# Set places for the side steps' matmuls, a rate of 2.9 for the second half's recurrence, one-pass spreads

## The chip, the cores and the metric

The kernel runs on one core of one Trainium2 chip. The metric is the device time of one launch in microseconds, here the median of three runs. The engines are named as in the profile: PE is the matrix engine, PEld its weight loads, DVE the vector engine, ACT the scalar engine, POOL GpSimd, SP the engine that issues many of the DMAs.

## The reference, cut to what matters

One inference step of two layers runs for a prompt of 1024 tokens and for eight sample streams of eight tokens. All weights are shared, all arithmetic is in float32.

```
layer 0:  h = rmsnorm(x);  z = h @ w_in0
          ya = short_conv(z[:, :1536])              # B * conv3(C * h)
          yb = rwkv7(z[:, 1536:])                   # token shift, decay, delta-rule state
          x += concat(ya, yb) @ w_out0
          x += (silu(n @ w_gate) * (n @ w_up)) @ w_down,  n = rmsnorm(x)
layer 1:  the same frame around forgetting attention (prompt, and eight decode streams
          over 2048 cached tokens in pages) and a Mamba-2 scan
y = rmsnorm(x)

rwkv7, per head and token:
          S = S * w_t - (S kk_t) (kk_t a_t)^T + v_t k_t^T ;   o_t = S r_t
          w_t from tanh(wd) @ w2,   a_t from ad @ a2          # two "lora" products, depth 64
```

## The kernel before, in words

The 1088 tokens are split into two halves: `H0` holds the 64 sample tokens and 512 prompt tokens, `H1` the other 512 prompt tokens. Activations lie with features on the partitions.

**Dense work.** A dense product is `gemm_tile` (8 blocks of the inner dimension), and for each block `mm3` (lines 202 to 206), which writes a nearly exact float32 product as three matmuls on rounded operands: high weights by high activations (L204), high by low (L205), low by high (L206). All three use the whole 128x128 array, with 320, 256 or 512 columns. `load_w` brings a weight tile by DMA, ACT rounds it (L196), and POOL or DVE forms the low part (L198).

**Side work.** The recurrence of layer 0 is cut into units of 256 tokens by 2 heads (class `Unit`: `prepare`, `core`, `finish`). Each is a long chain of small matmuls that go back and forth with DVE and ACT. In `core` a triangular matrix is inverted in blocks: `each` (L639) issues 16 matmuls of 32x32 on 16 places of the array, and DVE reads the result. In `prepare`, `small` (L539, L540) makes the lora products: L539 on the whole array and the correction L540 on 64 of its rows. In layer 1 the side work is attention (L1165, L1184, L1192), the paged decode (`decode`: scores L1254 with 128x32 weights, products with the values L1311) and the scan (`ssd`).

**How they are put together.** Both kinds are Python generators. `weave` (lines 485 to 495) takes one step of the dense generator, then as many steps of the side generator as the rate says; what is traced later has a later priority. A scheduler then goes through all instructions: among those that are ready by its own model of the engines it takes the one with the earliest priority, and so fixes the order on every engine. On the chip each engine runs its instructions in that order, and PE has one order for dense and side matmuls.

The weaves, in order: the first half's projection with a norm; `first` (short convolution of `H0`, projection of `H1`) with `recurrence(H0)` at rate 5.5; `second` (output projection and feed-forward of `H0` in layer 0) with `recurrence(H1)` at rate 6; then, in layer 1, `third` and an output feed-forward with attention, scan and decode at rate 1.8; and the last feed-forward with the norms at rate 1.

**Spreads.** A per-token factor that lies on partitions is broadcast and transposed to columns by a float32 matmul against the identity: L255 in `rms`, L838 in `Unit.finish`, L1221 in `decode`. A float32 matmul shows as two records in the trace, one for each of its passes; a matmul on rounded operands, or a transpose (L671), shows as one.

Of the kernel before, what the change touches and what calls it, by code (L numbers as in the profile page):

```python
# [34 lines left out]
CDEC = math.exp(-0.5)  # L35
NEG = -1e30

RATE = (5.5, 6, 1.8, 1.8, 1)

QY = 2  # L40
VY = 3
# [159 lines left out]

def mm3(k, acc, wh, wl, xh, xl, first, last):
    mm = k.nc.tensor.matmul
    mm(acc, wh, xh, start=first, stop=False)  # L204
    mm(acc, wh, xl, start=False, stop=False)  # L205
    mm(acc, wl, xh, start=False, stop=last)  # L206

# [19 lines left out]
def rms(k, H, xs, width, groups=None, ft=None, tag="acc"):  # L227

    nc = k.nc
    ft = ft or (lambda: k.ft(H))  # L230
    groups = groups or H.groups
    lo, hi = groups[0][0], groups[-1][1]
    blocks = [b for b in H.blocks if lo <= b[1] < hi]
    ss = ft()[:, lo:hi]
    for i, x in enumerate(xs):
        sq = ft()[:, lo:hi] if i else ss
        nc.scalar.activation(sq, x[:, lo:hi], AF.Square)  # L237
        if i:
            nc.vector.tensor_add(ss, ss, sq)  # L239
        if i % 2:  # L240
            yield
    pt = k.bank(tag)
    nb = len(blocks)
    for j, (l, _, _) in enumerate(blocks):
        nc.tensor.matmul(pt[:, j:j + 1], ss[:, l - lo:l - lo + P], k.con("ones"), start=True, stop=True)  # L245
    r = k.bp.tile([P, 16], F32, name="rs", tag="rs", bufs=2)
    nc.vector.tensor_scalar(r[:, 8:8 + nb], pt[:, :nb], 1.0 / width, EPS, op0=ALU.mult, op1=ALU.add)
    rsqrt(k, r[:, 0:nb], r[:, 8:8 + nb])
    yield
    out = []  # L250
    for a, b in groups:
        pb = k.bank(tag)
        for j, (_, c, w) in enumerate(blocks):
            if a <= c < b:
                nc.tensor.matmul(pb[:, c - a:c - a + w], r[:, j:j + 1].to_broadcast([P, P]), k.con("ident")[:, :w], start=True, stop=True)  # L255
        out.append((a, b, pb[:, :b - a]))
    yield
    return out
# [22 lines left out]
class Even:  # L281
    def __init__(self, k, pool):
        nc, A = k.nc, k.A
        self.k, self.mp = k, pool
        self.st_sc = pool.tile([P, 4, 16], F32, name="st_sc")
        nc.sync.dma_start(self.st_sc, A["st_sc"])
        self.st_shift = pool.tile([P, 14, 8], F32, name="st_shift")
        nc.sync.dma_start(self.st_shift, A["st_shift"])
        self.o_sc = pool.tile([P, 4, 18], F32, name="o_sc")
        nc.gpsimd.memset(self.o_sc, 0.0)  # L290
        self.o_shift = pool.tile([P, 14, 9], F32, name="o_shift")
        nc.gpsimd.memset(self.o_shift, 0.0)
        k.load_con(pool, 1)

        self.lora = [pool.tile([P, 512], F32R, name="lora%d" % i) for i in range(3)]
        raw = self.tile([P, 512], "up")
        for i, t in enumerate(self.lora):
            for c in range(2):
                nc.sync.dma_start(raw[64 * c:64 * c + 64], A["lora"][64 * (i if i < 2 else c):64 * (i if i < 2 else c) + 64])
            nc.scalar.copy(t, raw)  # L300
            if i == 2:
                nc.vector.tensor_sub(t, raw, t)
        self.g2 = pool.tile([P, 512], F32, name="g2")
        nc.sync.dma_start(self.g2, A["rw_g2"])
        self.reset = pool.tile([P, 512], F32, name="reset")
        nc.sync.dma_start(self.reset, A["resets"][0:1, 0:512].to_broadcast([P, 512]))
        self.dv = pool.tile([P, 30], F32, name="dv")
        dv = self.dv
        nc.vector.tensor_scalar(dv[:, 0:14], k.pp[:, PP["mu"]:PP["mu"] + 14], -1.0, 1.0, op0=ALU.mult, op1=ALU.add)
        for o, n, f in ((14, "w0", 0.5), (18, "a0", 0.5), (22, "ka", 0.5), (26, "kk", -0.5)):  # L310
            nc.vector.tensor_scalar(dv[:, o:o + 4], k.pp[:, PP[n]:PP[n] + 4], f, None, op0=ALU.mult)
        self.krz = [pool.tile([P, 4, 128], F32, name="krz%d" % h) for h in range(2)]
        for h in range(2):
            nc.gpsimd.memset(self.krz[h][64 * (1 - h):64 * (2 - h)], 0.0)
        self.state = []
        for p in range(4):
            s = pool.tile([P, 64], F32, name="S", tag="S%d" % p, bufs=2)
            nc.gpsimd.memset(s, 0.0)
            self.state.append(s)
# [162 lines left out]
        yield  # L482


def weave(dense, side, rate, rest=True):

    due = 0.0
    for _ in dense:
        due += rate
        while due >= 1:  # L490
            due -= 1
            if next(side, True) and not rest:
                return
    if rest:
        drain(side)
# [6 lines left out]
class Unit:  # L502
# [18 lines left out]
    def prepare(self):  # L521
# [8 lines left out]
        def small(c):  # L530

            z = la if c == 0 else self.et("la")
            nc.sync.dma_start(z[:, :n], k.zl[self.H.i][c][:, self.ts])
            z = z[:, :n].bitcast(F32R)
            o = k.bank()
            hs = slice(64 * c, 64 * c + 64)
            for sl, i in cols:
                f = slice(128 * i, 128 * i + 128)
                mm(o[:, sl], m.lora[c][:, f], z, start=True, stop=False)  # L539
                mm(o[:, sl], m.lora[2][hs, f], z[hs], start=False, stop=True)  # L540
            return o

        for j, x in ((1, xk), (0, xr), (2, xv)):
# [266 lines left out]
    def finish(self):  # L810
# [24 lines left out]
        yield  # L835
        pr = k.bank()
        for j in range(2):
            mm(pr[:, 128 * j:128 * j + 128], s2[:, 128 * j:128 * j + 128], k.con("ident"), start=True, stop=True)  # L838
        for sl, i in cols:
            V.scalar_tensor_tensor(oo[:, sl], oo[:, sl], k.col("lnw", i), pr[:, sl], op0=ALU.mult, op1=ALU.mult)  # L840
        yield
# [82 lines left out]
class Odd:  # L924
# [271 lines left out]
    def decode(self):  # L1196
# [6 lines left out]
        with k.tc.tile_pool(name="fd", bufs=1) as dp:  # L1203
# [7 lines left out]
            for p in range(4):  # L1211
                d = slice(32 * p, 32 * p + 32)
                sm = [tl([P, NS], "sm", 3) for _ in range(3)]
                for t, src in zip(sm, (k.qd, k.kd, k.vd[0])):
                    nc.sync.dma_start(t, src[p][:, 0:NS])
                for r in range(4):
                    e = slice(32 * r, 32 * r + 32)
                    V.tensor_copy(ksp[d, r], sm[1][e])
                    V.tensor_copy(qsp[d, r, :, p], by8(sm[0][e]))
                pt = k.bank()  # L1220
                mm(pt[0:64, 0:128], sm[2], k.con("ident"), start=True, stop=True)  # L1221
                S.copy(vs[:, 128 * p:128 * p + 128], pt[0:64, 0:128])
            cq = tl([P, 4], "cq")
            ncn = tl([P, NS], "ncnr")
# [292 lines left out]
def hybrid_step(tc, A, O):  # L1517
    nc = tc.nc
    k = K()
    k.nc, k.tc, k.A, k.O, k.cc = nc, tc, A, O, {}  # L1520
    k.low = nc.gpsimd
    with ExitStack() as es:
        cp = es.enter_context(tc.tile_pool(name="cp", bufs=1))
        dp = es.enter_context(tc.tile_pool(name="dp", bufs=1, space=DRAM))
# [33 lines left out]
        with tc.tile_pool(name="m0", bufs=1) as mp, tc.tile_pool(name="mps", bufs=1, space=PSUM) as k.mps:  # L1558
            norm = rms_split(k, H0, x0, "nm0")
            next(norm)  # L1560
            m = Even(k, mp)
            h0 = drain(norm)
            h1 = []

            def first():
                yield from m.short_conv(H0, h0)
                yield from m.project(H1, h1)
                yield from islice(conv1, CF[0])

            def norm1():  # L1570
                h1.extend((yield from rms_split(k, H1, x_in(H1), "nm0")))

            weave(m.project(H0, h0), norm1(), 1)
            x0 = []
            conv1 = m.short_conv(H1, h1)

            def second():
                x0.extend((yield from ffn0(H0, islice(conv1, CF[1]))))

            weave(first(), m.recurrence(H0), RATE[0])  # L1580
            weave(second(), m.recurrence(H1), RATE[1])
            h0 = drain(beside(rms_split(k, H0, x0, "nm1"), conv1))
            drain(conv1)
            m.finish()
        with tc.tile_pool(name="m1", bufs=1) as mp, tc.tile_pool(name="mps1", bufs=1, space=PSUM) as k.mps:
            m = Odd(k, mp)
            drain(m.dense(H0, h0))

            x2 = []

            def third():
                x1 = yield from ffn0(H1)
                h = yield from rms_split(k, H1, x1, "nm1")
                yield from m.dense(H1, h)

            ffn = keep(out_ffn(k, F0, 1), x2)
            k.low = nc.vector
            side = chain(m.latency(H0), m.latency(H1))
            weave(third(), side, RATE[2], False)
            weave(ffn, side, RATE[3], False)  # L1600
            k.low = nc.gpsimd
            drain(side)
            m.finish()
        with tc.tile_pool(name="x1", bufs=1) as k.xp:
            ffn1 = out_ffn(k, F1, 1, last=lambda xs, a, b: final(F1, xs, [(a, b)]))
            weave(ffn, islice(ffn1, 20), RATE[4])
            weave(ffn1, final(F0, x2), 1)


def scratch(k, dp):  # L1610
# [122 lines left out]
```

## Time and profile before

| | |
|---|---|
| median of three runs | 3324.24 us (3321.57 to 3326.07) |
| the profiled execution's own time | 3320.28 us |
| its span | 3318.5 us |
| PE busy | 3133.4 us, 94% of the span, 25213 records |
| PE weight loads | 2652.5 us, 80% |
| DVE busy | 1901.8 us, 57% |
| ACT busy | 1056.3 us, 32% |
| POOL busy | 839.8 us, 25% |
| mean granted clock of PE | 0.972 |

PE is the busiest engine by far, and the other engines serve it. Busy time says little of how well PE is used: matmuls are pipelined, so the records of neighbours overlap, and what a matmul costs is read from its start to the start of the next one.

### The profile page before, as it was taken

What the parts mean: (1) busy time and instruction counts of PE and PEld (TensorE: products, weight loads), DVE (VectorE), ACT (ScalarE), POOL (GpSimd) and SP (SyncE); (2) the same over time, 40 slices, a digit from 0 to 9 for tenths busy, and PEclk for the clock granted to TensorE, in tenths of its full rate; (3) what the DMA queues carried; (4) which work ended last, traced back from release to release, by engine and by line L of the source; (5) the groups of instructions that cost most, each with busy time, mean ns of one, the idle gap of its engine ahead of it and who ended that gap; (6) DMA issues with size and microseconds to landing.
All of it is one profiled execution on the core that took longest, in us unless ns stands there. A gap on an engine that the chain in (4) does not pass through costs nothing. (4 is left out here: it accounts for less than half of the span.)

```text
span 3318.5 us, 63244 instructions
## 1 busy us (share of the span) xinstructions
PE 3133.4 (94%) x25213; PEld 2652.5 (80%) x25213; DVE 1901.8 (57%) x3603; ACT 1056.3 (32%) x2083; POOL 839.8 (25%) x561
## 2 busy tenths in 40 slices
PE   7999999999999998999999998989999998999998
PEld 6877657777889997987677775766777776899998
DVE  6766646565544447566666466565545666544445
ACT  4333323332222223345322223332224553322222
POOL 3423333332323333310400103002010002433332
PEclk9999999999999998999999998999999998999999
DMA  5312233211112234643445656875544334232222
GB/s 179 117 59 80 88 92 122 68 60 56 57 61 83 83 104 128 212 153 102 144 143 167 203 155 209 252 225 176 171 166 148 111 106 152 70 109 83 82 80 78
DMA packets 238471, 409.20 MB, mean 123 GB/s; under 512 B 37632, under 2 KB 129664, under 8 KB 238176
## 3 DMA queue, kind: packets, MB, share of 16 engines
q10 hardware_dynamic: 63232, 218.80, 20.3%
q1 hardware_dynamic: 165584, 152.27, 15.4%
q0 software_dynamic: 9360, 34.08, 3.0%
q8 instruction: 199, 3.26, 0.4%
q14 instruction: 96, 0.79, 0.1%
HBM read 352.23 MB, written 52.81 MB: 122 GB/s over the span
## 5 line engine op out<-in xcount | busy, mean ns | idle before, releaser
L204 PE MATMUL acc<-hh,wh 128*128 128x320 f32 (+2 forms) x3720 | 1264.1, 341 | 19.0 <-ACT hh L218 15.3
L206 PE MATMUL acc<-hh,wl 128*128 128x320 f32 (+2 forms) x3720 | 1255.4, 338 | 6.3 <-POOL wl L198 6.2
L205 PE MATMUL acc<-hl,wh 128*128 128x320 f32 (+2 forms) x3720 | 1256.5, 338 | 4.6 <-DVE hl L219 3.6
L198 POOL TENSOR_TENSOR wl<-wraw,wh 128x1024 fp32r<-128x1024 f32 x225 | 540.1, 2401 | 1011.2 <-ACT wh L196 957.8
L204 PEld LDWEIGHTS acc<-hh,wh 128*128 128x128 f32 x3720 | 713.4, 192 | 98.9 <-ACT hh L218 20.5
L196 ACT CAST wh<-wraw 128x1024 fp32r<-128x1024 f32 (+1 forms) x398 | 416.0, 1045 | 1142.0 <-PE acc L205 1036.0
L205 PEld LDWEIGHTS acc<-hl,wh 128*128 128x128 f32 x3720 | 715.2, 192 | 70.4 <-DVE hl L219 6.9
L206 PEld LDWEIGHTS acc<-hh,wl 128*128 128x128 f32 x3720 | 714.6, 192 | 69.8 <-POOL wl L198 8.3
L903 DVE TENSOR_TENSOR x<-x,acc 128x320 f32<-128x320 f32 (+2 forms) x528 | 270.5, 528 | 142.5 <-PE acc L206 141.2
L205 PE MATMUL acc<-hidl,wh 128*128 128x320 f32 (+2 forms) x1056 | 352.0, 334 | 0.2 <-DVE hidl L219 0.2
L204 PE MATMUL acc<-hidh,wh 128*128 128x320 f32 (+2 forms) x1056 | 347.8, 336 | 3.8 <-ACT hidh L218 1.9
L206 PE MATMUL acc<-hidh,wl 128*128 128x320 f32 (+2 forms) x1056 | 348.6, 332 | 0.0
L198 DVE TENSOR_TENSOR wl<-wraw,wh 128x1024 fp32r<-128x1024 f32 x173 | 211.0, 1220 | 135.6 <-ACT wh L196 127.1
L1318 POOL DMA_INDIRECT kv<-in_cv,vidx x64 | 74.0, 1156 | 619.8 <-DMA kv<-in_ck 487.8
L204 PEld LDWEIGHTS acc<-hidh,wh 128*128 128x128 f32 x1056 | 198.7, 189 | 26.6 <-ACT hidh L218 4.5
L205 PEld LDWEIGHTS acc<-hidl,wh 128*128 128x128 f32 x1056 | 199.6, 189 | 18.0 <-issue 1.4
L206 PEld LDWEIGHTS acc<-hidh,wl 128*128 128x128 f32 x1056 | 199.8, 189 | 15.5 <-issue 1.0
L219 DVE TENSOR_TENSOR hidl<-ft,hidh 128x512 fp32r<-128x512 f32 (+2 forms) x148 | 177.1, 1196 | 57.0 <-ACT hidh L218 52.7
L891 DVE SCALAR_TENSOR_TENSOR ft<-ft,acc 128x320 f32<-128x320 f32 (+2 forms) x132 | 70.1, 531 | 205.9 <-PE acc L206 205.7
L885 DVE SCALAR_TENSOR_TENSOR ft<-ft,acc 128x320 f32<-128x320 f32 (+2 forms) x132 | 69.7, 528 | 177.7 <-ACT ft L884 177.6
L218 ACT CAST hidh<-ft 128x512 fp32r<-128x512 f32 (+2 forms) x148 | 75.2, 508 | 117.8 <-DVE ft L891 114.7
L1430 POOL TENSOR_TENSOR ac<-ac,bc 128x576 f32<-128x576 f32 (+1 forms) x16 | 27.2, 1710 | 292.2 <-DMA wraw<-in_wg 256.3
(344 smaller groups left out, 3314.1 us busy)
## 6 DMA issues: line engine op xcount, KB each, us to landing
wraw<-in_wi ACTq DMA_DIRECT2D x100, 512.0 KB
wraw<-in_wg ACTq DMA_DIRECT2D x88, 512.0 KB
wraw<-in_wu ACTq DMA_DIRECT2D x88, 512.0 KB
wraw<-in_wd ACTq DMA_DIRECT2D x88, 512.0 KB
kv<-in_ck SPq DMA_DIRECT2D x512, 64.0 KB
wraw<-in_wo ACTq DMA_DIRECT2D x32, 512.0 KB
ka<-kp SPq DMA_DIRECT2D x48, 128.0 KB
x<-in_xT SPq DMA_DIRECT2D x16, 288.0 KB
```

Source lines behind the costliest of these rows:

```text
L196: nc.scalar.copy(wh, raw)
L198: k.low.tensor_sub(wl, raw, wh)
L204: mm(acc, wh, xh, start=first, stop=False)
L205: mm(acc, wh, xl, start=False, stop=False)
L206: mm(acc, wl, xh, start=False, stop=last)
L218: k.nc.scalar.copy(hh, v)
L219: (eng or k.nc.vector).tensor_sub(hl, v, hh)
L885: nc.vector.scalar_tensor_tensor(s[:, a:b], s[:, a:b], 1.0, pc, op0=ALU.add, op1=ALU.mult)
L891: nc.vector.scalar_tensor_tensor(s[:, a:b], s[:, a:b], 0.5, pu, op0=ALU.mult, op1=ALU.mult)
L903: nc.vector.tensor_add(xs[n][:, a:b], xs[n][:, a:b], acc[:, :b - a])
L1318: nc.gpsimd.indirect_dma_start(out=v, out_offset=None, in_=A["cv"].rearrange("o (s r) c -> (o s) (r c)", r=2), in_offset=bass.IndirectOffs ...
L1430: G.tensor_mul(t, t, bc[2 + g])
```

## The change

`mm3` now notes each first matmul in `k.log`. `weave` asks, after each dense step, how many priorities it took (`back`) and which first matmuls it logged (`new`). If n side steps are due, the j-th is traced with its priorities moved back to the start of that dense step, and its PE instructions are put in the order behind the logged matmul number len(new)*j/n. That is an order on PE's queue alone, with no semaphore. The rate of the second half's recurrence goes from 6 to 2.9.

The correction of the lora products gets a fourth tile: tiles 2 and 3 hold the low part in their own 64 rows and zeros in the other 64, so that L540 uses all 128 rows. The three spreads become transposes.

```
-RATE = (5.5, 6, 1.8, 1.8, 1)
+RATE = (5.5, 2.9, 1.8, 1.8, 1)
...
-    mm(acc, wh, xh, start=first, stop=False)
+    k.log.append(mm(acc, wh, xh, start=first, stop=False))
...
-                nc.tensor.matmul(pb[:, c - a:c - a + w], r[:, j:j + 1].to_broadcast([P, P]), k.con("ident")[:, :w], start=True, stop=True)
+                nc.tensor.transpose(pb[:, c - a:c - a + P], r[:, j:j + 1].to_broadcast([P, P]), k.con("ident"))
...
-def weave(dense, side, rate, rest=True):
+def weave(k, dense, side, rate, rest=True):
...
     due = 0.0
-    for _ in dense:
+    while True:
+        p0, n0 = k.tc.cur_priority, len(k.log)
+        if next(dense, True):
+            break
+        back, new = k.tc.cur_priority - p0, k.log[n0:]
         due += rate
-        while due >= 1:
-            due -= 1
-            if next(side, True) and not rest:
+        n = int(due)
+        due -= n
+        for j in range(n):
+            with k.tc.issue_after(new[len(new) * j // n].ins) if new else nullcontext(), k.tc.high_priority(offset=back):
+                over = next(side, True)
+            if over and not rest:
                 return
...
-                mm(o[:, sl], m.lora[2][hs, f], z[hs], start=False, stop=True)
+                mm(o[:, sl], m.lora[2 + c][:, f], z, start=False, stop=True)
...
-            mm(pr[:, 128 * j:128 * j + 128], s2[:, 128 * j:128 * j + 128], k.con("ident"), start=True, stop=True)
+            nc.tensor.transpose(pr[:, 128 * j:128 * j + 128], s2[:, 128 * j:128 * j + 128], k.con("ident"))
...
-                mm(pt[0:64, 0:128], sm[2], k.con("ident"), start=True, stop=True)
+                nc.tensor.transpose(pt[0:64, 0:128], sm[2], k.con("ident"))
```

In the order of the built programs, PE comes to a matmul on a part of the array (a "small tile") out of other work 553 times before and 1252 times after the change; the number of dense matmuls, 14328, and of side matmuls, 5861, is the same. By line (numbers of the kernel before): L639 from 109 to 562, L1254 from 31 to 152, L1311 from 40 to 97, L540 from 40 to none, and all other lines from 333 to 441. The last matmul of the second half's recurrence stood behind 3198 dense matmuls and now stands behind 5257; `second` ends with the 5352nd.

On PE, in the second half's recurrence, before (L639 is one level of the block inverse, on tile `rk`; the rows with `acc` are the dense product around it):

```order
L204 MATMUL acc_6859<-hh_6485,wh_6827 128x256
L205 MATMUL acc_6859<-hl_6493,wh_6827 128x256
L639 MATMUL rk_6641<-t0_6639,nt_6621 32x32 x16
L206 MATMUL acc_6859<-hh_6485,wl_6829 128x256
L204 MATMUL acc_6993<-hh_6478,wh_6987 128x320
```

The same kind of level on PE in the changed program, later in the feed-forward (L652 is the former L639):

```order
L204 MATMUL acc_11728<-hidh_11310,wh_11724 128x320
L652 MATMUL rk_11794<-t0_11792,nt_11575 32x32 x3
L205 MATMUL acc_11728<-hidl_11311,wh_11724 128x320
L652 MATMUL rk_11794<-t0_11792,nt_11575 32x32
L206 MATMUL acc_11728<-hidh_11310,wl_11726 128x320
L652 MATMUL rk_11794<-t0_11792,nt_11575 32x32
L204 MATMUL acc_11728<-hidh_11482,wh_11724 128x320
L652 MATMUL rk_11794<-t0_11792,nt_11575 32x32
L205 MATMUL acc_11728<-hidl_11483,wh_11724 128x320
```

The 16 matmuls stood together between two dense matmuls; now dense and side matmuls take turns. Other levels still stand together.

On PE, in the paged decode, before (L1254 makes the scores of one page, on tile `fs`):

```order
L206 MATMUL acc_21624<-hh_17606,wl_21622 128x512
L1254 MATMUL fs_21588<-kt_21679,qsp_19152 32x128 x8
L1254 MATMUL fs_21588<-kt_21616,qsp_19152 32x128 x8
L204 MATMUL acc_21705<-hh_17599,wh_21699 128x512
L205 MATMUL acc_21705<-hl_17607,wh_21699 128x512
```

And in the changed program (L1267 is the former L1254):

```order
L204 MATMUL acc_21329<-hh_17609,wh_21325 128x512
L1267 MATMUL fs_21293<-kt_21384,qsp_19157 32x128
L205 MATMUL acc_21329<-hl_17617,wh_21325 128x512
L1267 MATMUL fs_21293<-kt_21384,qsp_19157 32x128
L206 MATMUL acc_21329<-hh_17609,wl_21327 128x512
L1267 MATMUL fs_21293<-kt_21384,qsp_19157 32x128
L204 MATMUL acc_21329<-hh_17610,wh_21325 128x512
```

Here too a page's scores went between two dense matmuls as a whole; now they take turns with them one by one. On the other engines the rows hardly change in number (DVE 3412 to 3431, ACT 2305 to 2307, POOL 551 to 546, SP 1969 to 1972).

## Rows read from the trace of the kernel before

**Rows 1.** The page, part 1: engine, busy us, share of the span, instructions.
```profile
PE 3133.4 (94%) x25213; PEld 2652.5 (80%) x25213; DVE 1901.8 (57%) x3603; ACT 1056.3 (32%) x2083; POOL 839.8 (25%) x561
```

**Rows 2.** Stretches of the three weaves with side work: length, busy, clock.
```profile
core 0: us, PE busy (x) PEld busy (x) DVE busy (x) ACT busy (x) POOL busy (x), PEclk, DMA share, GB/s
127.80:512.60 384.80, 359.12 (x4774) 274.52 (x4773) 238.79 (x622) 121.72 (x325) 125.48 (x110) 0.96 0.29 86
512.60:1242.80 730.20, 696.98 (x7138) 625.07 (x7137) 385.87 (x838) 202.38 (x431) 239.45 (x147) 0.98 0.23 75
...
1411.10:2838.40 1427.30, 1359.24 (x8163) 1047.67 (x8162) 856.77 (x1404) 492.06 (x926) 181.01 (x150) 0.97 0.52 163
```

**Rows 3.** Timeline, second weave, one small matmul between dense ones: start, us, instruction.
```profile
607.26 0.31 PE L205 MATMUL acc<-hl,wh 128*128 128x320 f32 x1
...
607.40 0.31 PE L206 MATMUL acc<-hh,wl 128*128 128x320 f32 x1
607.64 0.24 PE L700 MATMUL rk<-tt,wm 32*32 32x32 f32 x2
...
608.16 0.32 PEld L700 LDWEIGHTS rk<-tt,wm 32*32 32x32 f32 x14 [0.16 <-issue]
608.16 0.43 PE L700 MATMUL rk<-tt,wm 32*32 32x32 f32 x14
```

**Rows 4.** Timeline of PE, second weave: a level of 16 matmuls that stand together.
```profile
595.48 0.45 PE L639 MATMUL rk<-t,nt 32*32 32x32 f32 x32
595.86 0.42 PE L204 MATMUL acc<-hh,wh 128*128 128x320 f32 x1
596.11 0.31 PE L205 MATMUL acc<-hl,wh 128*128 128x320 f32 x1
```

**Rows 5.** Timeline of PE, decode: one 128x64 matmul between dense ones.
```profile
1696.72 0.40 PE L205 MATMUL acc<-hidl,wh 128*128 128x512 f32 x1
1696.96 0.40 PE L206 MATMUL acc<-hidh,wl 128*128 128x512 f32 x1
1697.29 0.43 PE L1221 MATMUL rk<-con,sm 128*64 128x128 f32 x2
1697.65 0.50 PE L204 MATMUL acc<-hidh,wh 128*128 128x512 f32 x1
```

**Rows 6.** Timeline of PE, decode: the 16 score matmuls of a page, together.
```profile
1748.19 1.08 PE L1254 MATMUL fs<-kt,qsp 128*32 128x128 f32 x32
1749.21 0.51 PE L204 MATMUL acc<-hh,wh 128*128 128x512 f32 x1
1749.55 0.39 PE L205 MATMUL acc<-hl,wh 128*128 128x512 f32 x1
```

**Rows 7.** Timeline of PE, decode: eight products with the values, together.
```profile
1881.58 1.07 PE L1311 MATMUL rk<-kv,pd 128*32 128x256 f32 x16
1882.58 0.50 PE L204 MATMUL acc<-hh,wh 128*128 128x512 f32 x1
```

**Rows 8.** Timeline of PE, first weave: a lora product and its correction.
```profile
306.64 0.28 PE L539 MATMUL rk<-la,lora 128*128 128x256 f32 x1
306.85 0.38 PE L540 MATMUL rk<-la,lora 64*128 64x256 f32 x1
...
307.50 0.40 PE L204 MATMUL acc<-hh,wh 128*128 128x512 f32 x1
```

**Rows 9.** Timeline of PE, first weave: float32 passes of 128 columns on the whole array.
```profile
303.27 1.16 PE L622 MATMUL rk<-krz,kb 128*128 128x128 f32 x8 [0.45 <-DVE o_shift L398]
304.27 1.06 PE L622 MATMUL rk<-kr,kb 128*128 128x128 f32 x8
```

**Rows 10.** Groups by line, PE, 127.8 to 2838.4 us: records | busy, mean ns | idle before.
```profile
L838 PE MATMUL rk<-con,s 128*128 128x128 f32 x68 | 12.1, 302 | 4.8 <-DVE s L834 3.7 <-ACT vu L682 0.9 <-DVE tt L665 0.3
```

**Rows 11.** Two stretches of 3.4 us in the second weave, columns as in Rows 2.
```profile
706.70:710.10 3.40, 1.96 (x65) 1.26 (x68) 3.40 (x9) 0.59 (x3) 1.03 (x1) 1.00 0.64 171
710.10:713.50 3.40, 3.40 (x69) 2.99 (x59) 1.64 (x8) 0.46 (x1) 0.00 (x0) 0.50 0.27 99
```

More of the change, by code (lines that the diff above doesn't have):

```diff
@@ L293, in __init__ @@
         k.load_con(pool, 1)
-        self.lora = [pool.tile([P, 512], F32R, name="lora%d" % i) for i in range(3)]
+        self.lora = [pool.tile([P, 512], F32R, name="lora%d" % i) for i in range(4)]
         raw = self.tile([P, 512], "up")
-        for i, t in enumerate(self.lora):
+        for i, t in enumerate(self.lora[:3]):
             for c in range(2):
@@ L301, in __init__ @@
             if i == 2:
-                nc.vector.tensor_sub(t, raw, t)
+                for c in range(2):
+                    hs = slice(64 * c, 64 * c + 64)
+                    nc.vector.tensor_sub(self.lora[2 + c][hs], raw[hs], t[hs])
+                nc.vector.memset(raw, 0.0)
+                for c in range(2):
+                    hs = slice(64 * c, 64 * c + 64)
+                    nc.scalar.copy(self.lora[3 - c][hs], raw[hs])
         self.g2 = pool.tile([P, 512], F32, name="g2")
@@ L535, in small @@
             o = k.bank()
-            hs = slice(64 * c, 64 * c + 64)
             for sl, i in cols:
@@ L1521, in hybrid_step @@
     k.low = nc.gpsimd
+    k.log = []
     with ExitStack() as es:
@@ L1571, in norm1 @@
                 h1.extend((yield from rms_split(k, H1, x_in(H1), "nm0")))
-            weave(m.project(H0, h0), norm1(), 1)
+            weave(k, m.project(H0, h0), norm1(), 1)
             x0 = []
@@ L1578, in second @@
                 x0.extend((yield from ffn0(H0, islice(conv1, CF[1]))))
-            weave(first(), m.recurrence(H0), RATE[0])
-            weave(second(), m.recurrence(H1), RATE[1])
+            weave(k, first(), m.recurrence(H0), RATE[0])
+            weave(k, second(), m.recurrence(H1), RATE[1])
             h0 = drain(beside(rms_split(k, H0, x0, "nm1"), conv1))
@@ L1598, in hybrid_step @@
             side = chain(m.latency(H0), m.latency(H1))
-            weave(third(), side, RATE[2], False)
-            weave(ffn, side, RATE[3], False)
+            weave(k, third(), side, RATE[2], False)
+            weave(k, ffn, side, RATE[3], False)
             k.low = nc.gpsimd
@@ L1605, in hybrid_step @@
             ffn1 = out_ffn(k, F1, 1, last=lambda xs, a, b: final(F1, xs, [(a, b)]))
-            weave(ffn, islice(ffn1, 20), RATE[4])
-            weave(ffn1, final(F0, x2), 1)
+            weave(k, ffn, islice(ffn1, 20), RATE[4])
+            weave(k, ffn1, final(F0, x2), 1)
 def scratch(k, dp):
```

## The prediction

> **What bounds the kernel now.** I read the busy table first, then the weaves as stretches, then the timeline of PE around single side matmuls, and last the clock. PE is busy for 94% of the span, the next engine for 80% (PE's own weight loads) and DVE for 57% [rows 1]: whatever lengthens PE's own queue lengthens the run, unless it fills time in which PE waits. How much of that there is, the stretches show [rows 2]: PE is idle for 384.8 - 359.1 = 25.7 us in the first weave with a recurrence, 33.2 in the second and 68.1 in layer 1, together 127 us. The granted clock there is 0.96, 0.98 and 0.97; at half clock half the time is lost, so the shortfalls 0.04 x 384.8, 0.02 x 730.2 and 0.03 x 1427.3 make 15 + 15 + 43 = 73 us. Waiting and slow clock are thus worth 200 us at most in the stretches that the change touches. Some waiting can hide in busy records, since the ends of matmuls are modelled; I keep that for the range.
>
> The decisive rows are those of one small matmul among dense ones. Two dense matmuls of 320 columns start 0.14 to 0.15 us apart (607.26, 607.40). Before a small one the distance is 0.24 (607.40 to 607.64). From there to the next small one, with one dense matmul between, it is 0.52 (607.64 to 608.16) [rows 3]. So one 32x32 matmul that stands alone costs 0.52 - 0.147 = 0.37 us of PE, with nothing waiting in it. Sixteen that stand together cost little more: 0.24 - 0.147 = 0.09 to get in, 0.38 to get back to a dense matmul, and 0.25 - 0.147 = 0.10 more on that one: 0.57 us [rows 3, 4]. PE pays for leaving the dense stream and coming back, not for the small matmuls.
>
> **The change part by part.** PE leaves for a small tile 553 times before and 1252 times after, 699 more, by the built order. For side matmuls on the whole array an extra place costs nothing that I can see, and I price none.
>
> 1. The block inverse (L639): 453 more. Sixteen alone cost 16 x 0.37 = 5.92 us against 0.57 together, 0.357 for each of the 15 that were added: 453 x 0.357 = +162 us. Bounds: the halves of a level, or three together, cost less for each; 0.30 gives 136, 0.37 gives 168.
>
> 2. The scores of the decode (L1254): 121 more. The trace has none alone; the nearest row is a 128x64 matmul of as many columns between dense ones of 512: in at 1696.96 to 1697.29 (0.33 against 0.24 for two dense ones, 0.09), 0.36 until the next dense one [rows 5], and 0.34 - 0.24 = 0.10 more on that [rows 6]: 0.55 us. Sixteen together cost 1.02 + 0.09 + 0.10 = 1.21 [rows 6]. That is (16 x 0.55 - 1.21) / 15 = 0.51 each, 121 x 0.51 = +62 us. If the narrower weights come in as fast as those of the 32x32 matmul, it is 0.37 alone and (5.92 - 1.21) / 15 = 0.31 each, +38.
>
> 3. The products with the values (L1311): 57 more, none alone in the trace. They have twice the columns of the 128x64 row, so at least its 0.55; eight together cost 1.00 + 0.19 [rows 5 to 7]. (8 x 0.55 - 1.19) / 7 = 0.46; I take 0.5, 57 x 0.5 = +28 us, between 0.3 and 0.65 (17 to 37).
>
> 4. The other small-tile lines: 333 entries before, 441 after, 108 more. They are mostly pieces of two to four matmuls, cheaper per piece: I take 0.3, +32 us, between 0 (they fall where PE waited) and 40.
>
> 5. The lora correction on all rows: 40 entries go. A product and its correction take from 306.64 to 307.50, 0.86 us, of which one dense matmul of 512 columns is 0.24 [rows 5, 8]; two of 256 columns on the whole array take at most two of the 320-column distances, 0.29. That is 0.33 saved, about 0.37 at 256 columns: 40 x 0.37 = -15 us; eight of them have only 64 columns, so -10 is the other bound. The zeros are written before the first weave, beside dense work: 0, at worst +2.
>
> 6. One-pass spreads: L838 shows 68 records for its 34 matmuls [rows 10], and the spreads of the norms lose 54 passes too. A pass of 128 columns on the whole array takes 1.00 us / 8 = 0.125 [rows 9]: 88 x 0.125 = -11 us; the four in the decode are within the rounding.
>
> Work added on PE: 162 + 62 + 28 + 32 - 15 - 11 = +258 us.
>
> 7. Waiting. The places are an order on PE's queue and no new wait: behind each side matmul stands a dense one. The chains get longer (a level of the inverse at one matmul per 0.52 us takes 8 us in place of 0.57), so DVE's reading of a level, and what stands behind it there, comes later. At the new pace there is room: the last matmul of that recurrence stands behind dense matmul 5257 of 5352, so nothing is left to drain. Of the idle time I give back three quarters in the second weave, whose pace is halved (-25 us), and a third in the other two, whose rates stay (-31); with some waiting that hides in busy records I take -70. Bounds: 0, and all 127. The clock I leave as it is: 0, between -73 and +60 (third rival).
>
> Sum on the profiled execution's own time: 3320.3 + 258 - 70 = 3508 us, of which the span is all but 2 us. The median of the runs is 4 us above that execution: 3512 us forecast.
>
> **The rivals.** *Faster: coming back costs nothing.* If weights for the next matmul are loaded while the last one streams, small and dense matmuls alternate freely, and only the gains are left: 3324 - 70 - 15 - 11 = 3228, and down to 3180 if more waiting goes. It decides if an alternating pair takes 0.15 + 0.05 us in place of 0.52. Against it: the weight load of L700 starts at 608.16 together with its matmul, 0.52 us behind the last start of that kind, and "issue" says that it waited for nothing that the profile shows; it was not pulled under the dense matmul [rows 3]. [...]
>
> *Even: waiting eats the whole cost.* If nearly all idle time and half of the slow clock go (-165), and the pieces fall at the lower ends (136 + 38 + 17 + 0 - 15 - 11 = 165), the time is 3324; at the middle prices it is 3417. For it: PE waits in just these stretches. Against it: the rates of two of three weaves are the same, and 127 us of idle is half of what is added.
>
> *Slower still: the clock falls in the alternating stretches.* There 453 periods of 0.52 and 178 of about 0.79 us (0.55 + 0.24) make 377 us in which PE streams few columns. The clock fell to half behind a stretch in which PE was at work for 1.96 of 3.40 us on small matmuls [rows 11]. If a third of the 377 us runs at half clock and half of each period scales with it, that is 377 / 3 x 0.5 = +63 us: 3575, and 3620 with no waiting recovered. [...]
>
> *The change does not do what it says:* if PE's order on the chip were another than the built one. Nothing speaks for it; PE runs its queue in order.
>
> **How the numbers follow.** The forecast, with its own bounds (terms 1 to 7 at their ends), 0.70, between 3430 and 3580. The clock falls, 0.14, 3575 to 3640. The even rival 0.11, 3317 to 3430; of this 0.02 lies within 0.2% of 3324 (3317.6 to 3330.9), which is about what a measurement of this kernel can tell from no change, and 0.01 below. The faster rival 0.05. So faster 0.06, same 0.02, slower 0.92. The range for 8 in 10 takes the forecast's bounds, most of the clock's case above and the upper part of the even one below: 3400 to 3615.
>
> **What would show it.** In the profile after: records of L652 of two at a time, alternating with dense rows at about 0.52 us from one to the next; the stretch of the second weave near 730 + 80 us, the first near 385 + 35, layer 1's near 1427 + 75; PE's idle time in them down by half, while PE's busy share rises above 94% though the run is longer. About 90 fewer records on PE. The prediction is wrong if alternating rows stand 0.2 to 0.3 us apart, or if the second weave is no longer than 760 us; its size is wrong if the granted clock leaves 0.95 to 0.99.

## The result, and the profile after

The changed kernel takes 3676.7 us (median of 4 runs, 3665.49 to 3691.95); the kernel before, timed beside it, 3325.15 (4 runs, 3321.57 to 3326.63). The ratio is 1.107 [1.104, 1.110]: 352 us slower, where 188 were forecast (3512), and outside the range given (3400 to 3615). The direction was right, the size was not.

The page of the changed kernel, engines and the row of the granted clock:

```profile
PE 3523.8 (96%) x25121; PEld 2817.5 (77%) x25121; DVE 1899.4 (52%) x3605; ACT 1064.5 (29%) x2085; POOL 835.6 (23%) x561
PEclk9977898988878888999989999899999999999999
```

PE has 92 records fewer than before [rows 1] and is busy 390 us longer; DVE, ACT and POOL do the same work as before. The clock row is the second thing to see: its sevens and most of its eights stand in the first 40% of the span, which is where the two recurrences run.

The stretches of the three weaves in the changed kernel (columns: length, busy time of each engine with its instructions, granted clock, DMA share, GB/s; the last row is layer 1):

```profile
128.30:594.10 465.80, 444.65 (x4777) 318.69 (x4775) 243.66 (x643) 128.44 (x334) 128.62 (x115) 0.87 0.24 74
594.10:1496.20 902.10, 888.37 (x7099) 735.36 (x7100) 377.01 (x830) 204.17 (x432) 240.64 (x146) 0.86 0.19 59
...
1662.40:3195.20 1532.80, 1469.34 (x8070) 1054.05 (x8069) 856.42 (x1400) 491.34 (x924) 170.41 (x149) 0.97 0.49 151
```

Against [rows 2] the first weave is 81 us longer (384.8 to 465.8) and the second 172 (730.2 to 902.1). Layer 1 now ends its stretch at an earlier dense matmul (8070 PE records against 8163); before, the stretch to the same matmul is this one:

```profile
1411.10:2829.20 1418.10, 1350.04 (x8094) 1038.47 (x8093) 850.63 (x1399) 490.43 (x924) 176.65 (x149) 0.97 0.52 163
```

so layer 1 is 115 us longer (1532.8 against 1418.1). PE's idle time in the three went from 25.7, 33.2 and 68.1 us to 21.2, 13.7 and 63.5. The clock went from 0.96 and 0.98 to 0.87 and 0.86 in the two recurrences, and stayed at 0.97 in layer 1.

### The profile page after: what moved, and what is told of

Same layout as the page of the kernel before. It is cut to its first block, busy times and chain, and to the rows that moved or that the text cites. A ratio compares the mean times of both kernels' runs of the same rounds, so it can differ in the third digit from the quotient of the medians.

```text
span 3682.6 us, 62973 instructions
## 1 busy us (share of the span) xinstructions
PE 3523.8 (96%) x25121; PEld 2817.5 (77%) x25121; DVE 1899.4 (52%) x3605; ACT 1064.5 (29%) x2085; POOL 835.6 (23%) x561
## 5 line engine op out<-in xcount | busy, mean ns | idle before, releaser
L205 PE MATMUL acc<-hl,wh 128*128 128x320 f32 (+2 forms) x3720 | 1318.7, 355 | 7.8 <-DVE hl L219 5.9
L204 PE MATMUL acc<-hh,wh 128*128 128x320 f32 (+2 forms) x3720 | 1300.4, 351 | 26.2 <-ACT hh L218 20.5
L206 PE MATMUL acc<-hh,wl 128*128 128x320 f32 (+2 forms) x3720 | 1299.8, 350 | 4.2 <-POOL wl L198 4.0
L204 PEld LDWEIGHTS acc<-hh,wh 128*128 128x128 f32 x3720 | 734.0, 198 | 110.9 <-ACT hh L218 25.1
L205 PEld LDWEIGHTS acc<-hl,wh 128*128 128x128 f32 x3720 | 733.3, 197 | 100.3 <-issue 24.8
L206 PEld LDWEIGHTS acc<-hh,wl 128*128 128x128 f32 x3720 | 734.0, 197 | 82.8 <-issue 19.8
L205 PE MATMUL acc<-hidl,wh 128*128 128x320 f32 (+2 forms) x1056 | 368.2, 349 | 0.5 <-DVE hidl L219 0.5
L206 PE MATMUL acc<-hidh,wl 128*128 128x320 f32 (+2 forms) x1056 | 364.3, 346 | 0.0
L204 PE MATMUL acc<-hidh,wh 128*128 128x320 f32 (+2 forms) x1056 | 359.9, 347 | 1.1 <-DVE x L916 0.5
L652 PEld LDWEIGHTS rk<-t,nt 32*32 32x32 f32 x2112 | 65.7, 112 | 85.2 <-issue 72.0
```

The lines of the kernel that those rows point to most:

```text
L204: k.log.append(mm(acc, wh, xh, start=first, stop=False))
L652: mm(o[q, 32 * c:32 * c + 32], lhs[q, c], rhs[q, c], start=True, stop=True)
```

## The experiments

All of them compute the full result. "Entries" are the times PE comes to a small tile out of other work, counted in the built order; by the count used for these runs the changed kernel has 1242 (1252 ahead of the prediction). A count of PE's records in the traces lies higher for every kernel but keeps the distances within a few: 1335 for the changed kernel, 599 for experiment 1 and 1371 for experiment 2, which are counted as 1242, 509 and 1278 here. In `weave`, a side step is given the scheduling priority that the dense step began with (`offset=back`), and that is undone behind each side step. So the side step whose place is at the first dense matmul has the same priorities as the dense matmuls themselves, one by one, and the scheduler lets them take turns; side steps with later places come out together.

The theory to test: the whole loss comes from taking turns, that is, from the price of an entry and from the clock that falls there. Under the rivals, the set places or the slower pace cost the time, whether or not the matmuls take turns.

**1. The same places and pace, with side matmuls together.**

```diff
-  ... k.tc.high_priority(offset=back):
+  ... k.tc.high_priority(offset=back + 300):
```

> The changed kernel with one number altered: the side steps' priorities go 300 further back than the start of the dense step, so that a side step's matmuls stand before the dense ones as soon as they are ready and behind their set place, and no longer take turns with them. PE comes to a small tile 509 times by the built order (553 before the change, about 1250 with it). Theory A (the cost is the taking of turns: about 0.36 us for each time PE leaves the dense stream, and the clock that falls in the alternating stretches): nothing of the loss is left, the granted clock is 0.96 or more in both recurrences, and the time is 3240 to 3310 us. Rival B (the cost comes from the moved priorities, which let side work on DVE, ACT and POOL pass the dense work's evictions and weight preparation): that is kept here, and the time stays above 3550. Rival C (the pace of 2.9 costs): also kept, above 3450.

Measured: 3296.01 us (3294.61 to 3299.04), ratio to before 0.993 [0.990, 0.995], with 509 entries. Its weaves (same columns):

```profile
129.90:517.50 387.60, 352.21 (x4779) 273.11 (x4777) 244.25 (x650) 127.77 (x339) 131.91 (x118) 0.96 0.29 91
517.50:1206.80 689.30, 673.73 (x7097) 613.01 (x7098) 382.57 (x823) 201.97 (x427) 237.49 (x143) 0.98 0.23 76
1373.20:2807.00 1433.80, 1350.15 (x8069) 1036.19 (x8068) 856.84 (x1400) 491.43 (x924) 167.20 (x149) 0.97 0.51 162
```

And PE's timeline around a level of the block inverse (start, length, instruction):

```profile
702.54 0.45 PE L652 MATMUL rk<-t,nt 32*32 32x32 f32 x32
702.92 0.41 PE L205 MATMUL acc<-hidl,wh 128*128 128x320 f32 x1
```

One number in the priorities takes away all of the loss, 381 us: the sixteen matmuls of a level stand together again, in one row of 32 records (two for each). The clock is back at 0.96 and 0.98, and the second weave is 41 us shorter than before [rows 2]. The rivals fell: neither the places nor the pace cost much. What the turns cost is 902.1 - 689.3 = 213 us in the second weave, 78 in the first and 99 in layer 1.

**2. Turns with three dense matmuls between lone small ones.** The changed kernel, with one line behind each small matmul of the block inverse:

```diff
     mm(o[q, 32 * c:32 * c + 32], lhs[q, c], rhs[q, c], start=True, stop=True)
+    k.tc.cur_priority += 2
```

> The changed kernel, with the priority moved on by two more after each 32x32 matmul of the block inverse: about as many lone small matmuls (1278 entries against about 1250), but most with three dense matmuls between them in place of one. Theory A, which puts 160 us of the loss down to the clock and the rest to leaving the dense stream: the granted clock of the two recurrences goes from 0.87 and 0.86 back to 0.94 or more, with the price of 0.36 us for each lone matmul still paid: 3500 to 3570 us. If the clock were a by-product of waiting and the whole loss were paid for leaving the dense stream (0.5 us and more for each): 3650 to 3700.

Measured: 3593.81 us (3580.43 to 3598.26), ratio 1.083 [1.080, 1.085], with 1278 entries, 36 more than in the changed kernel. Its two recurrences, and its timeline of PE:

```profile
127.50:548.50 421.00, 397.50 (x4758) 287.50 (x4758) 243.98 (x633) 129.23 (x335) 128.21 (x113) 0.98 0.26 80
548.50:1394.30 845.80, 824.89 (x7118) 677.10 (x7117) 384.37 (x840) 203.31 (x431) 239.87 (x147) 0.98 0.20 64
```

```profile
703.43 0.24 PE L652 MATMUL rk<-t,nt 32*32 32x32 f32 x2
703.61 0.50 PE L205 MATMUL acc<-hl,wh 128*128 128x512 f32 x1
703.95 0.39 PE L206 MATMUL acc<-hh,wl 128*128 128x512 f32 x1
704.18 0.39 PE L204 MATMUL acc<-hh,wh 128*128 128x512 f32 x1
704.50 0.24 PE L652 MATMUL rk<-t,nt 32*32 32x32 f32 x2
```

Most of the lone matmuls now have three dense ones between them, as these do. The clock is 0.98 in both, and no entry was saved. That separates the two parts. The price of an entry, from this run and the first: (3593.8 - 3296.0) / (1278 - 509) = 0.387 us, an average over all kinds of entries, net of the waiting that they fill. The clock: the changed kernel is 82.9 us slower than this one with 36 entries fewer, 82.9 + 36 x 0.387 = 97 us. The run is 24 us over the upper end of what was expected.

**3. Turns with two dense matmuls between.** The same line with `+= 1`.

> As the kernel that leaves three dense matmuls between lone 32x32 matmuls, with two (1315 entries to small tiles, 635 in the block inverse). [...] If the clock only follows the number of entries: 0.87 as in the changed kernel, and 3680 to 3720 us.

Measured: 3636.14 us (3632.78 to 3649.9), ratio 1.096 [1.094, 1.099], 1315 entries. Its recurrences:

```profile
127.20:577.90 450.70, 426.80 (x4778) 308.44 (x4776) 245.32 (x645) 128.73 (x335) 131.49 (x115) 0.92 0.25 77
577.90:1445.00 867.10, 855.78 (x7097) 692.48 (x7098) 378.22 (x829) 203.29 (x430) 238.03 (x145) 0.94 0.19 61
```

With one, two and three dense matmuls between, the second weave's clock is 0.86, 0.94 and 0.98. The author's estimate ahead of the run was a clock of 0.95 or more and 3590 to 3625 us if the second dense matmul were enough; the run came out between that and the time by entries alone. At 0.387 an entry it stands 3636.1 - 3593.8 - 37 x 0.387 = 28 us above the run with three: the part of the clock that is still lost.

**4. All side steps take turns.**

```diff
-  ... k.tc.high_priority(offset=back):
+  ... k.tc.high_priority(offset=back - back * j // n):
```

> The changed kernel with every side step's priorities starting at its own set place, so that nearly all of them take turns with the dense matmuls: 1818 entries to small tiles against about 1250, 902 in the block inverse against 562. The suspected cost, raised. Theory A: 340 more lone 32x32 matmuls at 0.385 us and as much again of the clock as the 453 cost (0.26 each), 219 us, and some 230 other entries at 0.3 to 0.5, 70 to 115: 3965 to 4010 us, granted clock of the recurrences at 0.80 or less. If PE hides entries beyond those that wait: below 3800.

Measured: 4060.52 us (4052.24 to 4073.33), ratio 1.224 [1.221, 1.226], 1818 entries. The second weave:

```profile
632.10:1839.80 1207.70, 1194.64 (x7097) 895.76 (x7098) 378.68 (x830) 203.41 (x430) 241.27 (x146) 0.74 0.13 44
```

The 576 entries more cost 384 us, 0.67 each, and the clock is 0.74. The run was expected at least 50 us lower. At 0.387 an entry the 576 make 223 us; the other 161 go with the clock, which fell in the second weave alone from 0.86 to 0.74. At the loss that is worked out below for half clock, that shortfall is (0.26 x 1207.7 - 0.14 x 902.1) / 0.5 x 0.36 = 135 us, an estimate. So the cost of taking turns rose faster here than their number (0.387, then 0.67 us an entry), and the clock fell with it (0.86 to 0.74).

**5. The changed kernel at the old pace** (`RATE[1]` 6 in place of 2.9).

> The changed kernel with the second half's rate back at 6 (one part undone). The built order has 984 entries to small tiles against about 1250, 310 of them in the block inverse against 562. Theory A: 252 fewer lone matmuls x 0.385 us = 97, and their share of the 118 us that the clock cost in the recurrences, 66, come off; some waiting returns: 3500 to 3560 us. Rival C (the pace is the loss): below 3400.

Measured: 3561.1 us (3551.39 to 3568.28), ratio 1.072 [1.070, 1.074], 984 entries, 1 us over the upper end of what was expected. At the higher rate more side steps have later places, and these stand together; hence fewer entries. Its two recurrences:

```profile
127.80:613.50 485.70, 463.43 (x4776) 330.27 (x4775) 243.99 (x643) 128.02 (x334) 129.03 (x115) 0.82 0.23 71
613.50:1377.40 763.90, 739.31 (x7099) 650.05 (x7100) 380.73 (x830) 203.56 (x432) 236.24 (x146) 0.94 0.21 69
```

The pace as the cause of the loss would have brought it under 3400, and falls. The first weave has the same order as in the changed kernel and yet took 20 us longer, at a clock of 0.82 against 0.87. So the clock's part is not a fixed sum: it differed between these two executions. Whether the chip has a part in that is open, since the record does not say on which chip the changed kernel ran; the four executions of this run, on one chip, spread over 17 us, with mean clocks from 0.943 to 0.952.

**6. Spreads and lora alone** (the old weave and pace, without set places).

```diff
-                nc.tensor.matmul(pb[:, c - a:c - a + w], r[:, j:j + 1].to_broadcast([P, P]), k.con("ident")[:, :w], start=True, stop=True)
+                nc.tensor.transpose(pb[:, c - a:c - a + P], r[:, j:j + 1].to_broadcast([P, P]), k.con("ident"))
...
-                mm(o[:, sl], m.lora[2][hs, f], z[hs], start=False, stop=True)
+                mm(o[:, sl], m.lora[2 + c][:, f], z, start=False, stop=True)
```

> The kernel before with two parts of the change alone: the lora correction on all 128 rows and the three one-pass spreads; weave and rates as before. 502 entries to small tiles against 553. Theory A, by the terms 5 and 6 of the prediction (-15 and -11 us): 3299 us, between 3285 and 3315. If PE's work there lay in waiting anyway: 3318 to 3325.

Measured: 3303.44 us (3298.3 to 3306.01), ratio 0.995 [0.993, 0.997]: 17 us faster, where terms 5 and 6 said 26, and within what was expected. The three weaves:

```profile
128.00:508.40 380.40, 349.15 (x4758) 267.93 (x4757) 240.74 (x622) 121.60 (x325) 125.27 (x110) 0.97 0.28 86
508.40:1227.20 718.80, 684.77 (x7115) 617.09 (x7114) 383.47 (x838) 202.37 (x431) 238.76 (x147) 0.98 0.23 76
1393.00:2810.00 1417.00, 1348.40 (x8070) 1034.65 (x8068) 851.97 (x1400) 490.59 (x924) 174.21 (x149) 0.97 0.52 164
```

PE is busy for 24 us less in them than in the kernel before (359.1 + 697.0 + 1350.0 against 349.2 + 684.8 + 1348.4), nearly the 26 of the forecast, and idle for 7 us more.

**7. The pace alone** (the kernel of experiment 6 with rate 2.9, old weave).

> As the kernel with the lora correction and the spreads alone, and with the rate of the second half's recurrence at 2.9; weave as before, with no set places and no moved priorities. 502 entries, the last matmul of that recurrence behind dense matmul 5304 of 5352. Theory A: the pace costs nothing by itself and gives back part of the 33 us of idle time and 15 us of slow clock in that stretch: 3260 to 3300 us, 0 to 35 below the kernel without the pace. Rival C (the pace costs): 3400 and more.

Measured: 3311.31 us (10 runs), ratio 0.998 [0.997, 0.999]. A miss: it was to be faster than experiment 6 and is 8 us slower. Its second weave:

```profile
509.60:1238.00 728.40, 685.18 (x7115) 620.70 (x7115) 385.98 (x838) 202.26 (x431) 238.51 (x147) 0.97 0.23 75
```

PE is just as busy as in experiment 6 and idle for 43 us in place of 34. What it waits for there (engine, tile and line, whom it waited for, total us, times, longest):

```profile
PE ch L754 <- DVE ys L729: 9.8, 8, 1.3
PE rk L682 <- DVE tt L670: 6.6, 4, 1.7
PE rk L544 <- DVE big L629: 6.4, 5, 1.3
```

These are links of the recurrence's own chain, eight or fewer times, one to two microseconds each. In the first experiment, same pace with set places, the longest entry of that view in the second weave is a wait of the dense product:

```profile
PE acc L205 <- DVE hl L219: 5.2, 2, 4.6
```

A slower pace does not take the chain's waits away by itself; it does so together with the places. Whether the places, with side matmuls together, would do it at the old pace was not run, so that the gain needs the slow pace is not shown; nor was it tried further why the pace alone lengthens the waits.

**8. Set places, kept together, only in the second recurrence** (the first experiment's weave for `second`, the old one for all others).

```diff
-            weave(k, first(), m.recurrence(H0), RATE[0])
+            weave_plain(k, first(), m.recurrence(H0), RATE[0])
             weave(k, second(), m.recurrence(H1), RATE[1])
...
-            weave(k, third(), side, RATE[2], False)
-            weave(k, ffn, side, RATE[3], False)
+            weave_plain(k, third(), side, RATE[2], False)
+            weave_plain(k, ffn, side, RATE[3], False)
...
```

> Set places with priorities far enough back that side matmuls stand together, but in the second weave alone; the other weaves as before the change. Pace, lora correction and spreads as changed. Theory A: where the rate is 2.9 the places give back waiting (the second weave took 689 us with them, 719 without places at the old pace, 728 without places at 2.9), and in the first weave (388 against 380) and layer 1 (1434 against 1417) they cost: 3303 - 30 = 3274 us, between 3262 and 3286, under both kernels. If the gain in the second weave only moves waiting to the next stretch: 3295 to 3305.

Measured: 3286.46 us (5 runs, 3273.39 to 3288.9), ratio 0.989 [0.987, 0.991]: faster than both kernels and the lowest time of all runs, though its interval touches that of experiment 1 (0.993 [0.990, 0.995]). It stands at the upper edge of what was expected.

```profile
127.50:519.50 392.00, 361.02 (x4759) 276.61 (x4757) 241.12 (x622) 121.64 (x325) 125.25 (x110) 0.93 0.27 85
519.50:1208.10 688.60, 673.18 (x7115) 611.97 (x7114) 387.64 (x838) 203.89 (x431) 241.04 (x147) 0.99 0.24 79
1373.20:2797.40 1424.20, 1355.42 (x8069) 1039.31 (x8068) 852.57 (x1399) 490.42 (x924) 173.42 (x149) 0.97 0.52 163
```

The second weave keeps its gain (688.6 against 718.8 in experiment 6). The first, in the code of experiment 6, took 380.4 there and 392.0 here, at a clock of 0.93 in this execution. In these runs set places helped only in the weave with the slow pace: in layer 1 the first experiment has 83.6 us of idle time (1433.8 - 1350.2), experiment 6 has 68.6.

## Why the prediction was right in direction and wrong in size

**Terms 1 to 4, the entries: right.** They forecast 162 + 62 + 28 + 32 = 284 us for 739 entries (699, and the 40 of the lora correction that term 5 counts). Between the first experiment and the second, entries cost 0.387 us each; 1242 - 509 = 733 of them make 284. That the two sums agree to the microsecond is luck: the forecast's price has the waiting that entries fill still in it, and the measured one has not. What was right are the single prices, and PE's timeline shows them. In the changed kernel, at full clock, in the block inverse and then in the decode:

```profile
1054.80 0.24 PE L652 MATMUL rk<-t,nt 32*32 32x32 f32 x2
1054.97 0.41 PE L206 MATMUL acc<-hh,wl 128*128 128x320 f32 x1
1055.31 0.24 PE L652 MATMUL rk<-t,nt 32*32 32x32 f32 x2
```

```profile
2192.84 0.41 PE L1267 MATMUL fs<-kt,qsp 128*32 128x128 f32 x2
2193.17 0.50 PE L205 MATMUL acc<-hl,wh 128*128 128x512 f32 x1
2193.61 0.41 PE L1267 MATMUL fs<-kt,qsp 128*32 128x128 f32 x2
2193.94 0.49 PE L206 MATMUL acc<-hh,wl 128*128 128x512 f32 x1
2194.36 0.41 PE L1267 MATMUL fs<-kt,qsp 128*32 128x128 f32 x2
```

From one lone matmul to the next (1054.80 to 1055.31) it is 0.51 us, against 0.52 in [rows 3]; in the decode 0.75 to 0.77, where 0.79 were forecast. One row of a lone matmul was enough to price the 453 of the block inverse at full clock.

**Terms 5 and 6: right in the work, too large in time.** 17 us were measured for the two, 26 forecast. The work went as forecast (PE is busy for 24 us less, experiment 6); 7 us of it came back as waiting.

**Term 7, the waiting: too large.** The prediction took three quarters of the second weave's idle time and a third of the rest, and something for waits hidden in busy records: 70 us. By the stretches 4.5 + 19.5 + 4.6 = 28.6 us came back. The weave with the slower pace did give back 19.5 of 33.2; but in the other two the places fill almost nothing. Whether any wait hid in busy records, the runs do not show.

**The step that failed: "The clock I leave as it is: 0, between -73 and +60".** It cost some 97 us (experiment 2), outside the bound. The rows of the changed kernel show what happens. The timeline as the clock falls, then stretches (columns as above):

```profile
1057.38 0.24 PE L652 MATMUL rk<-t,nt 32*32 32x32 f32 x2
1057.55 0.46 PE L205 MATMUL acc<-hl,wh 128*128 128x320 f32 x1
1057.94 0.31 PE L652 MATMUL rk<-t,nt 32*32 32x32 f32 x2
1058.18 0.64 PE L206 MATMUL acc<-hh,wl 128*128 128x320 f32 x1
1058.75 0.31 PE L652 MATMUL rk<-t,nt 32*32 32x32 f32 x2
1058.99 0.64 PE L204 MATMUL acc<-hh,wh 128*128 128x320 f32 x1
1059.55 0.31 PE L652 MATMUL rk<-t,nt 32*32 32x32 f32 x2
```

```profile
1054.40:1057.80 3.40, 3.40 (x25) 2.11 (x21) 2.55 (x2) 1.07 (x2) 2.36 (x1) 1.00 0.00 0
1057.80:1061.20 3.40, 3.40 (x14) 1.89 (x14) 0.07 (x1) 0.00 (x0) 0.00 (x0) 0.50 0.45 154
...
1064.60:1068.00 3.40, 3.40 (x43) 3.23 (x43) 1.02 (x3) 0.17 (x1) 0.00 (x0) 0.50 0.02 5
```

Up to 1057.8 the granted clock is 1.00, then 0.50, though PE's records leave no gap: 3.40 of 3.40 us. A period grows from 0.51 to 0.80 (1058.75 to 1059.55). In the last stretch a whole level stands together (32 of the 43 records), and behind it PE has dense matmuls alone:

```profile
1064.71 0.65 PE L652 MATMUL rk<-tt,wm 32*32 32x32 f32 x32
1065.29 0.64 PE L205 MATMUL acc<-hl,wh 128*128 128x320 f32 x1
1065.72 0.47 PE L206 MATMUL acc<-hh,wl 128*128 128x320 f32 x1
1065.99 0.47 PE L204 MATMUL acc<-hh,wh 128*128 128x320 f32 x1
```

The clock is still 0.50, and they start 0.27 us apart (1065.72, 1065.99) in place of 0.147: part of the loss falls on work that takes no turns at all. No idle time of PE stands ahead of the fall; its records cover the whole of each period, the time in which it comes to a tile and leaves it included.

The third rival had the mechanism and a chance of 0.14. Its price was too low, above all in how long the clock is low. It let a third of 377 us run at half clock, 126 us by their length at full clock. The shortfalls of the two recurrences, 0.13 x 465.8 + 0.14 x 902.1 = 187 against 30 us in the first experiment, mean 157 / 0.5 = 314 us at half clock, some 200 by their length at full clock, dense matmuls behind the turns included. It let a period grow by half, while it grew by 0.29 of 0.51, 57%. (Its upper figure is a slip besides: 3575 with no waiting recovered is 3575 + 70 = 3645, not 3620.) By the rows, a period of 0.80 in place of 0.51 loses 36% of its time, and 314 x 0.36 = 113 us, an estimate; the medians gave 97. (Half of the time, as the prediction counts the loss at half clock, is more than the rows show: dense matmuls behind one another lose 46%, 0.27 us in place of 0.147.) In the two profiled executions the changed kernel's recurrences are 465.8 - 421.0 + 902.1 - 845.8 = 101 us longer than those of experiment 2, and its 36 entries fewer make that 115.

[rows 11] alone could not settle this rival: in the stretch ahead of the fall PE was idle for 3.40 - 1.96 = 1.44 us, so the small matmuls and the waiting stand there together. The same trace has a row that keeps them apart. In the first weave the clock fell behind a stretch in which PE was busy for 4.38 of 4.50 us:

```profile
381.40:385.90 4.50, 4.38 (x83) 3.43 (x82) 2.76 (x6) 1.63 (x2) 2.24 (x1) 1.00 0.02 4
385.90:389.30 3.40, 3.40 (x10) 2.62 (x10) 2.87 (x10) 1.40 (x5) 1.08 (x3) 0.50 0.65 183
```

By the clock records of the traces it is the only one of 27 falls in the three weaves before; ahead of each of the others PE was idle for more than 1 us of 5. In the changed kernel 31 of 50 falls have no idle time of PE in the 5 us ahead of them.

**The sum again.** Entries 284, terms 5 and 6 at -17, clock +97 make 364; the rest of the first experiment's gain, 3303.4 - 3296.0 = 7 us, makes it 357, against 352 measured. Against the forecast's 188, the clock explains 97 of the difference, the waiting 63 (its share is -7 here, since the 0.387 is already net of what the turns fill) and terms 5 and 6 another 9; together that is 5 us more than the difference of 164.

**By stretch.** For the second weave, the first and layer 1, +80, +35 and +75 were forecast, and +172, +81 and +115 measured. The two recurrences are where the clock fell. Layer 1, where it stayed at 0.97, is off by 40: its idle time was hardly touched (68.1 to 63.5), and its set places, together, add 17 us against experiment 6 (1433.8 against 1417.0; experiment 8, with the old weave there, has 1424.2). Of the signs that the prediction named, 92 records fewer and periods of 0.51 us came; PE's idle time fell by 29 of 127 us and not by half; and the granted clock left 0.95 to 0.99, which was named as the sign that the size is wrong. The other rivals fell: two lone 32x32 matmuls with a dense one between never start less than 0.51 us apart in the changed kernel, and its rows on the chip take turns as in the built order (1054.80 to 1055.31 above: one matmul of L652, one dense one, one of L652).

## What to carry to other kernels

Price a reordering of TensorE's queue by how often it comes to a small tile, and take that price from one lone small matmul in the trace before: 0.37 us in [rows 3], against 0.387 an entry between experiments 1 and 2, with the clock at 0.96 to 0.98. Then ask of every stretch whose mix of work changes whether the granted clock would stay, and give that its own term and a range as wide as the loss at half clock (0.80 us a period here, in place of 0.51), even when the new order leaves no idle time: 31 of 50 falls came without any in the changed kernel. A place to start and the right to take turns are two things: the same places with the side matmuls kept together turned +352 us into a gain of 25 by the medians (0.993 [0.990, 0.995]), and confined to the recurrence with the slow pace, into 34 (0.989 [0.987, 0.991]).

## What the runs showed of the hardware that was not expected

- The granted clock fell from 1.00 to 0.50 in a stretch in which PE's records left no gap (3.40 of 3.40 us), and stayed at 0.50 into the dense matmuls behind, which then started 0.27 us apart in place of 0.147. Of the 50 falls in the three weaves of the changed kernel, 31 have no idle time of PE in the 5 us ahead.
- The clock went with the mix: lone 32x32 matmuls with mostly one, two and three dense ones between gave a clock of 0.86, 0.94 and 0.98 in the second weave. Layer 1, where score matmuls of 128 columns on 32 columns of the array take turns with dense ones of 512, kept the 0.97 that it had before.
- At half clock a period of a dense and a lone small matmul took 0.80 us (1058.75 to 1059.55) in place of 0.51 (1054.80 to 1055.31), not twice as long.
- The clock of the same order differed between executions: 0.87 and 0.82 in the first weave of the changed kernel and of experiment 5, 0.97 and 0.93 in that of experiments 6 and 8. Experiments 6 and 8 ran on different chips, and for the changed kernel the chip is not on record, so a part of the chip in this is not excluded.
